# Pair jobs of a streaming-encoder layer: the last half-block sum reads its PSUM bank through VectorE, without a ScalarE copy in between

## The chip, the core and the metric

The kernel runs on one core of a Trainium2 chip. The engines of that core that matter here are TensorE (PE, with its weight loads shown apart as PEld), VectorE (DVE), ScalarE (ACT) and GpSimd (POOL); loads are issued by SyncE (SP) and GpSimd. Each engine works through its own queue in order and waits on semaphores of the others. The metric is the device time of one execution in microseconds, the median of several runs. A profile is of one execution; its span goes from the first to the last instruction.

## What is computed

One layer of an encoder for a sequence of 512 tokens of width 1024: a feed-forward block (FFN 1), a mixer with a recurrent and an attention branch, and a second feed-forward block (FFN 2), with RMS norms around each.

```python
f = swiglu(rms_norm(h, ffn1_pre_g[l]), ffn1_w1[l], ffn1_w3[l], ffn1_w2[l])
h = h + 0.5 * rms_norm(f, ffn1_post_g[l])
u = rms_norm(h, mix_pre_g[l])
q, k, v, xr, xg = jnp.split(u @ w_in[l], splits, axis=-1)
...
y_a = (hr * jax.nn.gelu(xg)) @ w_lru_out[l]
...
g = jax.nn.sigmoid(u @ w_gate[l] + b_gate[l]).reshape(b, s, N_BRANCHES, d)
...
f = swiglu(rms_norm(h, ffn2_pre_g[l]), ffn2_w1[l], ffn2_w3[l], ffn2_w2[l])
h = h + 0.5 * rms_norm(f, ffn2_post_g[l])

def swiglu(x, w1, w3, w2):
    return (jax.nn.silu(x @ w1) * (x @ w3)) @ w2
```

All inputs and outputs are float32. The kernel splits each operand of a product into a high and a low part that TensorE takes in a narrower form of float32, so every product is three matmuls: high x high, low x high, high x low.

## The kernel before

Feature-major products (weights stationary, tokens moving) of a block of 128 features take eight contraction blocks of 128. In most of FFN 1 and FFN 2, in the gelu projection `xg` and in the last two blocks of the gate projection `wg`, two blocks of features are made together as a **pair job**. A job treats the two feature blocks, the two halves of the contraction and the two halves of the tokens as a 2 x 2 matrix product and forms it with seven products instead of eight, each a call of `mm_s` (4 contraction blocks x 3 = 12 matmuls of 128 x 256). Sums of weight blocks are made ahead (S12, S34, by GpSimd or VectorE), sums of the tokens' blocks once per stage (t1 to t4).

The class `Pairs` runs the jobs of FFN 1 (18, w1 and w3 in turn) and FFN 2 (20), `GeluPairs` the four of `xg`, `GatePairs` the one of `wg`: 43 in all. A job holds three PSUM banks, of eight there are:

- `bu` takes a11, and ScalarE copies it out as `q1`; then s2 is added to it, and ScalarE copies that out as `u`; then s3 is added; last, **a22** is added, and what it holds then becomes the left half of the second output block.
- `bx` takes s1, copied out as `q5` by ScalarE; then s4 is added.
- `bc` takes a12.

VectorE makes three sums of them into the job's output tile `c`: bc + q1 (L953), bx + u (L958), and what `bu` holds after s3, plus q5 (L965, in the other two classes L1039 and L1111). `q1`, `q5`, `u` and `v` are quarters of one tile `ct`.

The order on every engine is the order in which the program is written; nothing reorders it. Within a job PE has a11, s1, **the a22 of the job before** (the function `last`), s2, a12, s4, s3. So between s3 and the a22 that adds to the same bank stand 24 matmuls: the a11 and s1 of the next job. In a stage's last job a12 comes after s3 and a22 right after that, so there 12 stand between. In VectorE's queue the third sum comes behind the split of S34 of the next job (`prep(n + 1, 3)`), in ScalarE's queue the copy `v` behind the high half of that split, and in a w3 job of FFN 1 behind the silu of the job before. `prep(n + 1, i)` makes the high parts on ScalarE and the low parts on VectorE (L226 and L227, `split2`).

Tiles come from one pool of 42 equal slots, so a new tile waits for whoever used its slot last. PSUM banks come from a ring of eight.

Of the kernel before, what the change touches and what calls it, by code (L numbers as in the profile page):

```python
# [12 lines left out]
AF = mybir.ActivationFunctionType  # L13
ALU = mybir.AluOpType

P = 128
# [35 lines left out]
def hybrid_layer(ctx: ExitStack, tc: tile.TileContext, a: dict, out: bass.AP):  # L52
    nc = tc.nc
    act, dve, pool, pe, sp = nc.scalar, nc.vector, nc.gpsimd, nc.tensor, nc.sync
# [8 lines left out]
    def slot(shape, dt=F32, name="s"):  # L63
        uid[0] += 1
        return sb.tile(shape, dt, tag="slot", name=f"{name}_{uid[0]}")
# [782 lines left out]
    class Pairs:  # L848
# [65 lines left out]
        def run(self, tail, hooks={}):  # L914
            X = self.X
            assert st["get"] == st["split"] == self.k0, (st, self.k0)
            st["get"] = st["split"] = self.k0 + 2 * len(self.jobs)
            last = silu = lambda: None
            for n, (nm, f) in enumerate(self.jobs):
                W = self.w.pop(n)  # L920
                first = nm == self.na
                tmp = slot([P, 4, 256], name="ct")
                q1, q5, u, v = (tmp[:, i, :] for i in range(4))
                c = slot([P, 2, SEQ], name="cc")
                if first:
                    self.c1[f] = c
                bu, bx, bc = (bank("c")[:, :256] for _ in range(3))
                at = lambda i: [f() for f in hooks.get((n, i), ())]
                mm_s(W["a11"], X["b11"], bu)
                act.activation(q1, bu, AF.Copy)  # L930
                at(1)
                mm_s(W["s1"], X["t1"], bx)
                act.activation(q5, bx, AF.Copy)
                at(2)
                if self.R is not None:
                    self.prep(n + 1, 1)
                silu = last() or silu
                self.prep(n + 1, 1)
                mm_s(W["s2"], X["t2"], bu, True)
                del W["s1"], W["s2"]  # L940
                act.activation(u, bu, AF.Copy)
                at(3)
                if n == len(self.jobs) - 1:
                    silu()
                    silu = lambda: None
                    if self.R is None:
                        tail()
                self.prep(n + 1, 2)

                def c11():  # L950
                    mm_s(W["a12"], X["b21"], bc)
                    del W["a11"], W["a12"]
                    dve.tensor_tensor(out=c[:, 0, :256], in0=bc, in1=q1, op=ALU.add)  # L953

                if n < len(self.jobs) - 1:
                    c11()
                mm_s(W["s4"], X["b22"], bx, True)
                dve.tensor_tensor(out=c[:, 0, 256:], in0=bx, in1=u, op=ALU.add)  # L958
                self.prep(n + 1, 3)
                silu()  # L960
                silu = lambda: None
                mm_s(W["s3"], X["t3"], bu, True)
                del W["s3"], W["s4"]
                act.activation(v, bu, AF.Copy)
                dve.tensor_tensor(out=c[:, 1, 256:], in0=v, in1=q5, op=ALU.add)  # L965
                if n == len(self.jobs) - 1:
                    tail()
                    if self.R is not None:
                        tail()
                    c11()  # L970
                if not first:
                    c1 = self.c1[f]
                    to = self.hid.f
                    to.update((f + i, self.hid.place(f + i, c1[:, i, :])) for i in range(2))
                    dve.tensor_tensor(out=to[f], in0=c1[:, 0, :], in1=c[:, 0, :], op=ALU.mult)
                    dve.tensor_tensor(out=to[f + 1][:, 256:], in0=c1[:, 1, 256:], in1=c[:, 1, 256:], op=ALU.mult)
                self.prep(n + 1, 4)
                self.prep(n + 2, 0)
                self.raws(n + 3)

                def last(W=W, bu=bu, c=c, f=f, first=first):
                    mm_s(W.pop("a22"), X["t4"], bu, True)
                    if first and self.R is not None:
                        act.activation(c[:, 1, :256], bu, AF.Copy)
                        dve.tensor_tensor(out=c, in0=c, in1=self.R, op=ALU.mult)
                        return lambda: act.activation(c, c, AF.Silu)
                    if first:
                        act.activation(c[:, 1, :256], bu, AF.Silu)
                        act.activation(c[:, 0, :], c[:, 0, :], AF.Silu)
                        act.activation(c[:, 1, 256:], c[:, 1, 256:], AF.Silu)  # L990
                    else:
                        c1 = self.c1.pop(f)
                        dve.tensor_tensor(out=self.hid.f[f + 1][:, :256], in0=bu, in1=c1[:, 1, :256], op=ALU.mult)

            last()

    class GeluPairs(Pairs):


        def run(self, scans, yh, yl, tail, between):  # L1000
            X, end = self.X, len(self.jobs) - 1
            assert st["get"] == st["split"] == self.k0, (st, self.k0)
            st["get"] = st["split"] = self.k0 + 2 * len(self.jobs)
            self.raws(2)
            last = mult = parts = lambda: None
            gelu = lambda v: act.activation(v, v, AF.Gelu_apprx_tanh)
            for n, (nm, f) in enumerate(self.jobs):
                W = self.w.pop(n)
                tmp = slot([P, 4, 256], name="ct")
                q1, q5, u, v = (tmp[:, i, :] for i in range(4))  # L1010
                c = slot([P, 2, SEQ], name="cc")
                bu, bx, bc = (bank("c")[:, :256] for _ in range(3))
                mm_s(W["a11"], X["b11"], bu)
                act.activation(q1, bu, AF.Copy)
                mm_s(W["s1"], X["t1"], bx)
                act.activation(q5, bx, AF.Copy)
                self.prep(n + 1, 1)
                between(n)
                last()
                mm_s(W["s2"], X["t2"], bu, True)  # L1020
                act.activation(u, bu, AF.Copy)
                mult()
                self.prep(n + 1, 2)

                def c11():
                    mm_s(W["a12"], X["b21"], bc)
                    dve.tensor_tensor(out=c[:, 0, :256], in0=bc, in1=q1, op=ALU.add)

                if n < end:
                    c11()  # L1030
                mm_s(W["s4"], X["b22"], bx, True)
                dve.tensor_tensor(out=c[:, 0, 256:], in0=bx, in1=u, op=ALU.add)
                parts()
                self.prep(n + 1, 3)
                if n == end:
                    tail()
                mm_s(W["s3"], X["t3"], bu, True)
                act.activation(v, bu, AF.Copy)
                dve.tensor_tensor(out=c[:, 1, 256:], in0=v, in1=q5, op=ALU.add)  # L1039
                if n == end:  # L1040
                    c11()
                gelu(c[:, 0, :])
                if n < end:
                    self.prep(n + 1, 4)
                    self.prep(n + 2, 0)
                self.raws(n + 3)

                def last(W=W, bu=bu, c=c):
                    mm_s(W["a22"], X["t4"], bu, True)
                    act.activation(c[:, 1, :256], bu, AF.Gelu_apprx_tanh)  # L1050
                    gelu(c[:, 1, 256:])

                def mult(c=c, f=f):
                    dve.tensor_tensor(out=c, in0=c, in1=scans[f // 2], op=ALU.mult)

                def parts(c=c):
                    yh.append(slot([P, 2, SEQ], F32R, name="yh"))
                    yl.append(slot([P, 2, SEQ], F32R, name="yl"))
                    split2(yh[-1], yl[-1], c)

            tail()
            last()
            mult()
            parts()

    class GatePairs(Pairs):


        def run(self, gz, bias, tail):
# [3 lines left out]
            last = lambda: None  # L1073
            for n, (nm, f) in enumerate(self.jobs):
                W = self.w[n]
                tmp = slot([P, 4, 256], name="ct")
                q1, q5, u, v = (tmp[:, i, :] for i in range(4))
                c = gz[f // 2] = slot([P, 2, SEQ], name="g")
                bu, bx, bc = (bank("c")[:, :256] for _ in range(3))

# [26 lines left out]
                    tail()  # L1107
                mm_s(W["s3"], X["t3"], bu, True, mark=False)
                del W["s3"], W["s4"]
                act.activation(v, bu, AF.Copy)  # L1110
                dve.tensor_tensor(out=c[:, 1, 256:], in0=v, in1=q5, op=ALU.add)  # L1111
                if n == end:
                    c11()
                gate(c[:, 0, :], 0, 0, SEQ)
# [821 lines left out]
```

## Time and profile before

| | us |
|---|---|
| median of 3 runs (1099.37 to 1099.71) | 1099.57 |
| span of the profiled execution | 1097.6 |
| median less span of the profiled execution | 1.97 |
| PE busy | 1089.0 |
| VectorE busy | 928.9 |
| ScalarE busy | 704.3 |
| GpSimd busy | 420.0 |
| the copies `v` of `Pairs` (38), ScalarE busy | 14.4 |
| the third sums of `Pairs` (38), VectorE busy | 31.3 |

The profiled execution has no device time of its own in the page beside the span; the difference to the median is what lies around the span. Matmuls overlap in the records and their ends are modelled, so the pace of PE is read from the distance between starts. A row of the timeline gives the start and the duration in us, engine, line, operation, output <- input, and in brackets how long the engine was idle before it and on what.

### The profile page before, as it was taken

How to read it: one execution, taken by the hardware profiler on the slowest of the kernel's cores; microseconds unless marked ns; L12 is line 12 of the kernel's file. 1: busy time of each engine (PE TensorE's matmuls, PEld its weight loads, DVE VectorE, ACT ScalarE, POOL GpSimd, SP SyncE). 2: the span in 40 equal slices, each digit the busy share in tenths (PEclk: the TensorE clock that was granted, in tenths of full speed). 3: DMA queues.
4: the chain of work that ended last, by engine and by line, in shares of the span. 5: the costliest groups of instructions: out<-in, count | busy, mean ns of one | idle time of the engine just before them, and what ended most of it. 6: DMA issues, size and time to landing. Idle time of an engine off the chain costs nothing.

```text
span 1097.6 us, 18111 instructions
## 1 busy us (share of the span) xinstructions
PE 1089.0 (99%) x6856; PEld 986.3 (90%) x6856; DVE 928.9 (85%) x1334; ACT 704.3 (64%) x1226; POOL 420.0 (38%) x352
## 2 busy tenths in 40 slices
PE   9999999999999999999999999999999999999997
PEld 7899999998889878899888888888999999998885
DVE  5887999989997998887778867767889989889996
ACT  7756555588767778656656654456555455578872
POOL 0043933232102513242556573010977656633200
PEclk9999999999999999999999999999999999999999
DMA  9325663389866752157132335452423323449923
GB/s 332 129 81 141 127 156 105 110 187 230 231 174 206 166 153 71 39 180 242 60 96 79 113 137 211 138 189 89 123 78 116 110 84 108 147 101 243 206 78 134
DMA packets 53895, 156.46 MB, mean 143 GB/s; under 512 B 5536, under 2 KB 7456, under 8 KB 53808
## 3 DMA queue, kind: packets, MB, share of 16 engines
q1 hardware_dynamic: 40272, 122.49, 33.0%
q0 software_dynamic: 13248, 32.29, 15.6%
q8 instruction: 54, 0.88, 0.3%
q10 hardware_dynamic: 288, 0.52, 0.2%
q14 instruction: 33, 0.27, 0.1%
HBM read 139.57 MB, written 13.62 MB: 140 GB/s over the span
## 4 chain that ended last, share of the span: by engine, by line
PE 99%; DMA 0%; DVE 0%; ACT 0%; issue 0%; DVEq 0%; SPq 0%; ACTq 0%
PE c L842 13%; PE c L843 13%; PE c L844 13%; PE f L237 10%; PE f L238 10%; PE f L239 9%; PE hw L734 6%; PE hw L732 6%; PE hw L733 6%; PE acc L255 1%; PE acc L257 1%; PE acc L256 1%; PE pt L1696 1%; PE s L1660 1%; PE s L1659 1%; PE tr L355 1%
## 5 line engine op out<-in xcount | busy, mean ns | idle before, releaser
L843 PE MATMUL c<-uT,wlo 128*128 128x256 f32 x516 | 146.0, 283 | 0.0
L844 PE MATMUL c<-uT,whi 128*128 128x256 f32 x516 | 146.0, 283 | 0.0
L842 PE MATMUL c<-uT,whi 128*128 128x256 f32 x516 | 146.0, 283 | 0.0
L842 PE MATMUL c<-Xh,whi 128*128 128x256 f32 x504 | 142.7, 283 | 0.0
L843 PE MATMUL c<-Xh,wlo 128*128 128x256 f32 x504 | 142.6, 283 | 0.0
L237 PE MATMUL f<-uT,whi 128*128 128x512 f32 (+1 forms) x380 | 138.5, 365 | 0.0
L238 PE MATMUL f<-uT,wlo 128*128 128x512 f32 (+1 forms) x380 | 136.9, 360 | 0.0
L239 PE MATMUL f<-uT,whi 128*128 128x512 f32 (+1 forms) x380 | 136.9, 360 | 0.0
L844 PE MATMUL c<-Xl,whi 128*128 128x256 f32 x456 | 129.1, 283 | 0.0
L227 DVE TENSOR_TENSOR wlo<-S,whi 128x1024 fp32r<-128x1024 f32 x86 | 121.1, 1408 | 5.9 <-POOL OL L1732 3.1
L226 ACT ACTIVATE whi<-S 128x1024 fp32r<-128x1024 f32 x86 | 88.5, 1054 | 29.8 <-DVE S L891 28.7
L843 PEld LDWEIGHTS c<-uT,wlo 128*128 128x128 f32 x516 | 99.0, 192 | 0.2
L842 PEld LDWEIGHTS c<-uT,whi 128*128 128x128 f32 x516 | 99.0, 192 | 0.2
L844 PEld LDWEIGHTS c<-uT,whi 128*128 128x128 f32 x516 | 99.0, 192 | 0.0
L842 PEld LDWEIGHTS c<-Xh,whi 128*128 128x128 f32 x504 | 96.8, 192 | 0.3 <-issue 0.3
L843 PEld LDWEIGHTS c<-Xh,wlo 128*128 128x128 f32 x504 | 96.8, 192 | 0.0
L732 PE MATMUL hw<-whi,uT 128*128 128x512 f32 x228 | 88.7, 389 | 0.0
L734 PE MATMUL hw<-whi,uT 128*128 128x512 f32 x228 | 88.7, 389 | 0.0
L844 PEld LDWEIGHTS c<-Xl,whi 128*128 128x128 f32 x456 | 87.5, 192 | 0.0
L733 PE MATMUL hw<-wlo,uT 128*128 128x512 f32 x216 | 84.0, 389 | 0.0
L237 PEld LDWEIGHTS f<-uT,whi 128*128 128x128 f32 x380 | 71.8, 189 | 12.1 <-issue 1.7
L239 PEld LDWEIGHTS f<-uT,whi 128*128 128x128 f32 x380 | 71.7, 189 | 11.0
(435 smaller groups left out, 3206.9 us busy)
## 6 DMA issues: line engine op xcount, KB each, us to landing
raw_w1b<-in_w1b_dram SPq DMA_DIRECT2D x22, 512.0 KB, 4.1
raw_w3b<-in_w3b_dram SPq DMA_DIRECT2D x22, 512.0 KB, 4.4
raw_w3a<-in_w3a_dram SPq DMA_DIRECT2D x21, 512.0 KB, 4.9
raw_w1a<-in_w1a_dram SPq DMA_DIRECT2D x20, 512.0 KB, 4.5
raw_w2a<-in_w2a_dram SPq DMA_DIRECT2D x17, 512.0 KB, 6.2
raw_wg<-in_wg_dram SPq DMA_DIRECT2D x16, 512.0 KB, 3.8
raw_w2a<-in_w2a_dram POOLq DMA_DIRECT2D x15, 512.0 KB, 10.2
raw_w2b<-in_w2b_dram SPq DMA_DIRECT2D x15, 512.0 KB, 6.1
```

Of the source, the lines that this page charges most:

```text
L226: act.activation(hi, src, AF.Copy)
L227: dve.tensor_tensor(out=lo, in0=src, in1=f32(hi), op=ALU.subtract)
L237: pe.matmul(ps[:, c0:c1], wh[:, s], h_, start=k == 0 and c0 == 0, stop=False, skip_group_check=True)
L238: pe.matmul(ps[:, c0:c1], wl[:, s], h_, start=False, stop=False, skip_group_check=True)
L239: pe.matmul(ps[:, c0:c1], wh[:, s], l_, start=False, stop=k == KT - 1, skip_group_check=True)
L255: pe.matmul(acc[n], x[:, 0, c], wh[:, s], start=first, stop=False, skip_group_check=skip)
L732: pe.matmul(ps, xs[:, 0, j, c], hi[:, j, :], start=start and j == 0, stop=False, skip_group_check=True)
L733: pe.matmul(ps, xs[:, 0, j, c], lo[:, j, :], start=False, stop=False, skip_group_check=True)
L734: pe.matmul(ps, xs[:, 1, j, c], hi[:, j, :], start=False, stop=i == self.G - 1, skip_group_check=True)
L842: pe.matmul(ps, wh[:, s], xh, start=first, stop=False, skip_group_check=True)
L843: pe.matmul(ps, wl[:, s], xh, start=False, stop=False, skip_group_check=True)
L844: pe.matmul(ps, wh[:, s], xl, start=False, stop=k == 3, skip_group_check=True)
```

## The change

The ScalarE copy of `bu` after s3 is gone, with the quarter `v` of the tile. VectorE's third sum reads the bank itself. This is done in all three classes.

```diff
@@ class Pairs @@
-                tmp = slot([P, 4, 256], name="ct")
-                q1, q5, u, v = (tmp[:, i, :] for i in range(4))
+                tmp = slot([P, 3, 256], name="ct")
+                q1, q5, u = (tmp[:, i, :] for i in range(3))
...
                 mm_s(W["s3"], X["t3"], bu, True)
                 del W["s3"], W["s4"]
-                act.activation(v, bu, AF.Copy)
-                dve.tensor_tensor(out=c[:, 1, 256:], in0=v, in1=q5, op=ALU.add)
+                dve.tensor_tensor(out=c[:, 1, 256:], in0=bu, in1=q5, op=ALU.add)
@@ class GeluPairs @@
-                tmp = slot([P, 4, 256], name="ct")
-                q1, q5, u, v = (tmp[:, i, :] for i in range(4))
+                tmp = slot([P, 3, 256], name="ct")
+                q1, q5, u = (tmp[:, i, :] for i in range(3))
...
                 mm_s(W["s3"], X["t3"], bu, True)
-                act.activation(v, bu, AF.Copy)
-                dve.tensor_tensor(out=c[:, 1, 256:], in0=v, in1=q5, op=ALU.add)
+                dve.tensor_tensor(out=c[:, 1, 256:], in0=bu, in1=q5, op=ALU.add)
@@ class GatePairs @@
-                tmp = slot([P, 4, 256], name="ct")
-                q1, q5, u, v = (tmp[:, i, :] for i in range(4))
+                tmp = slot([P, 3, 256], name="ct")
+                q1, q5, u = (tmp[:, i, :] for i in range(3))
...
                 mm_s(W["s3"], X["t3"], bu, True, mark=False)
                 del W["s3"], W["s4"]
-                act.activation(v, bu, AF.Copy)
-                dve.tensor_tensor(out=c[:, 1, 256:], in0=v, in1=q5, op=ALU.add)
+                dve.tensor_tensor(out=c[:, 1, 256:], in0=bu, in1=q5, op=ALU.add)
```

The order of the instructions shows it at two places of FFN 1. First VectorE around the third sum of a w3 job, before and now; `c_` are PSUM banks, `ct` the tile of q1, q5 and u, `S` the sums of weight blocks, and in brackets stand the engines whose semaphore the row waits for (the number behind the name is the semaphore's own).

```order
L890 TENSOR_TENSOR S_244_1451<-raw_w1a_229_1327,S_243_1450 128x512 [waits Pool_49]
L891 TENSOR_TENSOR S_244_1451<-raw_w1a_229_1327,raw_w1a_230_1329 128x512 [waits DMAHW7_49]
L227 TENSOR_TENSOR wlo_1531<-S_243_1450,whi_1530 128x1024 [waits PE_49,Activation_49]
L953 TENSOR_TENSOR cc_1459<-c_1462,ct_1458 128x256 [waits PE_49]
L958 TENSOR_TENSOR cc_1459<-c_1461,ct_1458 128x256 [waits PE_49]
L227 TENSOR_TENSOR wlo_1561<-S_244_1451,whi_1560 128x1024 [waits Activation_49]
L965 TENSOR_TENSOR cc_1459<-ct_1458 128x256 [waits Activation_49]
L975 TENSOR_TENSOR hEO_1316<-cc_1332,cc_1459 128x512 [waits DVE_49]
```

```order
L890 TENSOR_TENSOR S_244_1444<-raw_w1a_229_1321,S_243_1443 128x512 [waits Pool_49]
L891 TENSOR_TENSOR S_244_1444<-raw_w1a_229_1321,raw_w1a_230_1323 128x512 [waits DMAHW7_49]
L227 TENSOR_TENSOR wlo_1524<-S_243_1443,whi_1523 128x1024 [waits Activation_49]
L953 TENSOR_TENSOR cc_1452<-c_1455,ct_1451 128x256 [waits PE_49]
L958 TENSOR_TENSOR cc_1452<-c_1454,ct_1451 128x256 [waits PE_49]
L227 TENSOR_TENSOR wlo_1554<-S_244_1444,whi_1553 128x1024 [waits Activation_49]
L964 TENSOR_TENSOR cc_1452<-c_1453,ct_1451 128x256 [waits PE_49]
L974 TENSOR_TENSOR hEO_1310<-cc_1326,cc_1452 128x512 [waits DVE_49,Activation_49]
```

The sum keeps its place in the queue; it now reads a bank and waits for PE in place of ScalarE. Lines behind it are one less in the changed file (two or three less in the later classes).

Second, PE where the a22 of that job begins (`Xh`, `Xl` are the split t4, `w` the split weight block a22), before and now:

```order
L842 MATMUL c_1725<-Xh_333,whi_1663 128x256
L843 MATMUL c_1725<-Xh_333,wlo_1664 128x256
L844 MATMUL c_1725<-Xl_334,whi_1663 128x256
L842 MATMUL c_1594<-Xh_549,w_258_1581 128x256 [waits Activation_49]
L843 MATMUL c_1594<-Xh_549,w_258_1581 128x256
L844 MATMUL c_1594<-Xl_550,w_258_1581 128x256
```

```order
L842 MATMUL c_1716<-Xh_333,whi_1655 128x256
L843 MATMUL c_1716<-Xh_333,wlo_1656 128x256
L844 MATMUL c_1716<-Xl_334,whi_1655 128x256
L842 MATMUL c_1586<-Xh_549,w_258_1573 128x256 [waits DVE_49]
L843 MATMUL c_1586<-Xh_549,w_258_1573 128x256
L844 MATMUL c_1586<-Xl_550,w_258_1573 128x256
```

PE's instructions stand as they stood; the first matmul of a22 waits for VectorE where it waited for ScalarE. Elsewhere the order of each engine is the same but for the missing copies, and some first writers of a slot wait for another engine than before, since slots come free in another order.

## The prediction

> **What bounds the kernel now.** I read the page first: busy shares, then the chain that ended last.
>
> ```profile
> span 1097.6 us, 18111 instructions
> ...
> PE 1089.0 (99%) x6856; PEld 986.3 (90%) x6856; DVE 928.9 (85%) x1334; ACT 704.3 (64%) x1226; POOL 420.0 (38%) x352
> ...
> PE 99%; DMA 0%; DVE 0%; ACT 0%; issue 0%; DVEq 0%; SPq 0%; ACTq 0%
> ```
>
> TensorE is both the busiest engine and the whole chain. A busy share can hide short gaps, so next I asked who PE waits for, and what one stretch of pair jobs looks like by windows.
>
> ```profile
> PE w L1152 <- POOL warm L1149: 1.1, 1, 1.1
> PE f L1202 <- ACT uT L1195: 0.4, 1, 0.4
> ...
> 82.50:110.00 27.50, 27.50 (x232) 27.50 (x231) 21.72 (x34) 18.10 (x28) 10.97 (x17) 1.00 0.55 141
> ```
>
> PE's listed waits come to 1.5 us in the whole run, all before the first result. In the window 232 matmuls fill 27.5 us, 119 ns each, at granted clock 1.00. So there is next to no waiting to win back: 1097.6 - 1089.0 = 8.6 us lie outside PE's busy time, in the ramp and after the last matmul, where the change has no instruction. What it can do is make PE wait. The question is therefore the slack of PE against the engine that reads the bank.
>
> **The change part by part.** It removes 43 ScalarE copies (38 + 4 + 1 jobs) and gives 43 VectorE adds a PSUM operand in place of an SBUF one. From the groups by shape, and two lines looked at alone (min/median/max ns):
>
> ```profile
> L964 ACT ACTIVATE ct<-c 128x256 f32<-128x256 f32 x38 | 14.4, 380 | 39.5 <-PE c L844 39.5
> L965 DVE TENSOR_TENSOR cc<-ct 128x256 f32<-128x256 f32 x38 | 31.3, 824 | 1.1 <-ACT ct L964 1.1
> ...
> L965 DVE TENSOR_TENSOR cc<-ct x38: 410/420/1522, 61.1 to 983.5; 128x256 f32<-128x256 f32 x38
> L953 DVE TENSOR_TENSOR cc<-c,ct x38: 404/412/420, 59.3 to 986.1; 128x256 f32<-128x256 f32 x38
> ```
>
> ScalarE loses 43 x 0.38 = 16 us of work, but it sat idle 39.5 us just before those copies, waiting for PE: worth nothing to the end by itself. The new add has the operands of L953 (a bank and ct), which takes 0.41 us every time; the old one took 0.41 to 1.52. So each add costs 0.41 us, at most 1.11 less than before and never more; over the 38 of this line 31.3 - 38 x 0.41 = 16 us less. The Trainium skill (Perfetto Trace Analysis, Optimizing Scalar/DVE Operations) gives VectorE about 60 ns of access overhead on SBUF and 125 on PSUM, and twice that in profiled latency: it speaks against the change, by an estimated 0.13 us per add, and with it the sum below would be about 0.9 us more. L953 against the median of L965 shows no such difference here.
>
> What the change moves is the release of bank bu. The last product of the job, a22 (written one job later), accumulates into bu; its first weight load waits until bu has been read. Before, the reader was ScalarE's copy; now it is VectorE's add, which stands in VectorE's queue behind the split of S34. Behind the waiting weight load stands all of PE's stream. The price of this wait is in the timeline:
>
> ```profile
> 5.72 0.75 DVE L1196 SCALAR_TENSOR_TENSOR uT<-xt,vec,uT 128x512 fp32r<-128x512 f32 x1 [0.40 <-ACT uT L1195]
> 6.53 0.19 PEld L1204 LDWEIGHTS f<-uT,whi 128*128 128x128 f32 x1 [0.49 <-DVE uT L1196]
> ...
> 152.58 0.36 ACT L964 ACTIVATE ct<-c 128x256 f32<-128x256 f32 x1
> ...
> 152.81 0.19 PEld L844 LDWEIGHTS c<-Xl,whi 128*128 128x128 f32 x1
> ...
> 152.99 0.19 PEld L842 LDWEIGHTS c<-Xh,w 128*128 128x128 f32 x1
> 153.05 0.33 PE L842 MATMUL c<-Xh,w 128*128 128x256 f32 x1
> ...
> 153.15 0.41 DVE L965 TENSOR_TENSOR cc<-ct 128x256 f32<-128x256 f32 x1
> ```
>
> The weight load at 6.53 starts 0.06 us after VectorE's 6.47 (its records at full precision: 0.05). At 152.99 the first load of a22 comes 0.18 after the load ahead of it, not 0.12, because the copy ended at 152.94: this job's bank is already released only just in time. And the add, which will now release it, does not end before 153.56. As a load normally starts 0.12 before its matmul, PE is held by (end of add - start of a22's matmul) + 0.05 + 0.12.
>
> Now the places where that is positive. I went through all 43 adds, put 0.41 in for each, and compared with the first matmul of its a22:
>
> ```profile
> 132.89 0.28 PE L842 MATMUL c<-Xh,w 128*128 128x256 f32 x1
> ...
> 132.99 0.41 DVE L965 TENSOR_TENSOR cc<-ct 128x256 f32<-128x256 f32 x1
> ...
> 173.25 0.28 PE L842 MATMUL c<-Xh,w 128*128 128x256 f32 x1
> ...
> 173.35 0.41 DVE L965 TENSOR_TENSOR cc<-ct 128x256 f32<-128x256 f32 x1
> ...
> 230.85 0.34 PE L842 MATMUL c<-Xh,w 128*128 128x256 f32 x1
> ...
> 231.12 0.42 DVE L965 TENSOR_TENSOR cc<-ct 128x256 f32<-128x256 f32 x1
> ...
> 492.02 1.51 DVE L1039 TENSOR_TENSOR cc<-ct 128x256 f32<-128x256 f32 x1
> ...
> 492.42 0.28 PE L842 MATMUL c<-Xh,w 128*128 128x256 f32 x1
> ...
> 509.69 0.42 DVE L1039 TENSOR_TENSOR cc<-ct 128x256 f32<-128x256 f32 x1
> ...
> 509.70 0.28 PE L842 MATMUL c<-Xh,w 128*128 128x256 f32 x1
> ...
> 946.67 0.41 DVE L965 TENSOR_TENSOR cc<-ct 128x256 f32<-128x256 f32 x1
> ...
> 946.75 0.28 PE L842 MATMUL c<-uT,w 128*128 128x256 f32 x1
> ```
>
> - FFN 1, three w3 jobs: 132.99 + 0.41 - 132.89 + 0.17 = **0.68**; the one at 153.05, of which 0.05 is already in the trace, **0.63**; 173.25 again **0.68**.
> - FFN 1, last job, where only c11 (12 matmuls) stands between: 231.54 - 230.85 + 0.17, less 0.06 already there (matmul 0.34 long in place of 0.28): **0.80**.
> - Gelu pairs: 492.43 - 492.42 + 0.17 = **0.18**; the last, again with c11 alone between: **0.58**.
> - FFN 2, one job: 947.08 - 946.75 + 0.17 = **0.50**.
>
> Do they add up, or does VectorE, once PE has stood still, have its lead back? That depends on whether VectorE's lag is tied to PE again in between:
>
> ```profile
> 123.01 0.38 ACT L933 ACTIVATE ct<-c 128x256 f32<-128x256 f32 x1 [1.05 <-PE c L844]
> 123.29 1.05 ACT L226 ACTIVATE whi<-raw_w1a 128x1024 fp32r<-128x1024 f32 x1
> ...
> 124.38 1.23 DVE L227 TENSOR_TENSOR wlo<-raw_w1a,whi 128x1024 fp32r<-128x1024 f32 x1 [0.82 <-ACT whi L226]
> ...
> 144.53 1.23 DVE L227 TENSOR_TENSOR wlo<-raw_w1a,whi 128x1024 fp32r<-128x1024 f32 x1 [0.58 <-ACT whi L226]
> ```
>
> Once per pair of jobs VectorE idles for a ScalarE half whose turn comes after q5, for which ScalarE waits on PE. A PE that is late shifts VectorE there by as much, and the lag builds up anew. So the stalls add. Two more places show a positive number, and drop out:
>
> ```profile
> 111.56 0.60 DVE L965 TENSOR_TENSOR cc<-ct 128x256 f32<-128x256 f32 x1 [0.83 <-ACT ct L964]
> ...
> 122.53 0.41 DVE L965 TENSOR_TENSOR cc<-ct 128x256 f32<-128x256 f32 x1
> ...
> 122.81 0.28 PE L842 MATMUL c<-Xh,w 128*128 128x256 f32 x1
> ...
> 502.50 0.28 PE L842 MATMUL c<-Xh,w 128*128 128x256 f32 x1
> 502.61 0.41 DVE L1039 TENSOR_TENSOR cc<-ct 128x256 f32<-128x256 f32 x1
> ```
>
> The first would cost 122.94 - 122.81 + 0.17 = 0.30, but the add before it no longer waits 0.83 us for a copy, and VectorE doesn't idle between the two; where it stalled all the same, the 0.68 at 132.89 would be that much less, as VectorE is tied to PE ahead of this a22. The second would cost 502.61 + 0.41 - 502.50 + 0.17 = 0.69, but the add before it (492.02) becomes 1.1 us shorter, which its successor should inherit.
>
> Sum: 0.68 + 0.63 + 0.68 + 0.80 + 0.18 + 0.58 + 0.50 = 4.05 us. Against the profiled execution's span this is 1097.6 + 4.05 = 1101.7; its median run is 1099.57, 1.97 above the span, so the time becomes **1103.6**. A stall of under a microsecond cannot be caught up later, as PE has no idle time to give.
>
> Bounds. Below: if the adds at all seven places come 0.7 us earlier than in this trace, nothing is left, 1099.6. Above: twelve further jobs lie within 0.1 us of the condition on one side or the other, for example
>
> ```profile
> 192.87 0.41 DVE L965 TENSOR_TENSOR cc<-ct 128x256 f32<-128x256 f32 x1
> ...
> 193.41 0.28 PE L842 MATMUL c<-Xh,w 128*128 128x256 f32 x1
> ```
>
> (193.28 - 193.41 + 0.17 = 0.04). The removed tile quarter and the vanished reader also alter which released buffer a later tile gets, so some GpSimd sums and loads start at other moments; one VectorE operation that falls on such a sum is 1.1 us longer (L965's 1.52 against 0.41). If that hits four of these jobs, 4 us come on top.
>
> **The rivals.**
> 1. *The stalls vanish: VectorE is relieved.* The adds that took 1.5 us now take 0.41. If that lead is carried to the seven adds, from 0.7 us on, the kernel stays at 1099.6. For it: the 16 us less of VectorE time. Against it: the relief lies in FFN 2 and Gelu, while the four FFN 1 places come after adds that took 0.41 already, with the tie to PE at 124.38 and 144.53 between. A half of the stalls (2 us, 1101.6) is still within what I call no change. 21%.
> 2. *The lag grows.* The shifted GpSimd sums fall on the split ahead of the add in the jobs that are within 0.1 us: 4.05 + 4 = 8 us, 1107.6. For it: the waits of several GpSimd sums do change. Against it: in FFN 1 after 134 us they don't. 18%.
> 3. *Faster.* ScalarE and VectorE together save some 32 us; if PE's pace of 119 ns held waits in it, the pair stages would shorten. At most the 1.5 us of listed waits could go, and they stand ahead of the first pair job: 1098.1 at best, or more only by a pace that no row here shows. 3%.
>
> **How the numbers follow.** The forecast, +3 to +5.5 us, has 58%; with rival 2 it makes slower 76%. Within 0.2% (2.2 us, about what a measurement of this kernel can tell from no change) is rival 1 with its half measure, 21%. The range runs from 1100.2 (a seventh of the stalls left) to 1107.2 (nearly all of rival 2); about 2 in 10 lie outside.
>
> **What would show it right or wrong.** Right: PE's waits list new entries on the add's line, some 0.5 to 0.8 us each, seven or so, near 133, 154, 174, 233, 495, 513 and 950 us (each later by the stalls ahead of it), with an unchanged 119 ns pace between; the add takes 0.41 us everywhere; ScalarE's busy time falls by 16 us, VectorE's by up to as much. Wrong: a first weight load of a22 that starts on time in the w3 jobs of FFN 1 (rival 1), stalls in many other jobs too (rival 2), or a PE wait on a load or a GpSimd sum, which I price at nothing.

## The result, and the profile after

| | before | after |
|---|---|---|
| median of 4 runs each on one chip, us | 1099.47 (1098.90 to 1099.71) | 1104.11 (1103.89 to 1104.34) |
| ratio, 95% interval | | 1.004 (1.0028 to 1.0053) |
| span of the profiled execution, us | 1097.6 | 1101.5 |
| VectorE busy, us | 928.9 | 911.9 |
| ScalarE busy, us | 704.3 | 689.5 |

The kernel became slower by 0.4%, 4.6 us, while two engines did some 32 us less work. The page of the changed kernel, in the same three lines as before:

```profile
span 1101.5 us, 18075 instructions
...
PE 1090.7 (99%) x6856; PEld 986.6 (90%) x6856; DVE 911.9 (83%) x1334; ACT 689.5 (63%) x1183; POOL 422.7 (38%) x352
...
PE 92%; DVE 5%; issue 1%; ACT 1%; DMA 0%; DVEq 0%; SPq 0%; ACTq 0%
```

The busy share of PE still reads 99%. The sign of a change is in the third of them: the chain that ended last now leaves PE and runs through VectorE for 5% of the span. That share is no cost. It says that PE was held by VectorE somewhere, and that the chain then follows VectorE's work back. The waits of PE say where (engine, line and tile that waited, what it waited for: total, times, longest):

```profile
PE c L842 <- DVE cc L964: 1.8, 4, 0.6
PE w L1149 <- POOL warm L1146: 1.1, 1, 1.1
PE f L1199 <- ACT uT L1192: 0.7, 1, 0.7
PE c L842 <- DVE cc L1037: 0.3, 1, 0.3
```

The second and third stand ahead of the first result and were there before (1.1 and 0.4 us). The first and the last are new: L842 is the first matmul of a product, L964 and L1037 are the sum that now reads the bank. Together they come to 2.1 us only, half of what was lost. The reason is seen in the timeline, at the first of these places (start, duration, instruction; in brackets the idle time ahead of it and what ended it):

```profile
132.10 1.21 DVE L227 TENSOR_TENSOR wlo<-S,whi 128x1024 fp32r<-128x1024 f32 x1
...
133.01 0.28 PE L844 MATMUL c<-Xl,whi 128*128 128x256 f32 x1
...
133.23 0.41 DVE L964 TENSOR_TENSOR cc<-c,ct 128x256 f32<-128x256 f32 x1
...
133.70 0.19 PEld L842 LDWEIGHTS c<-Xh,w 128*128 128x128 f32 x1 [0.61 <-DVE cc L964]
...
133.70 0.39 PE L842 MATMUL c<-Xh,w 128*128 128x256 f32 x1 [0.41 <-DVE cc L964]
133.92 0.28 PE L843 MATMUL c<-Xh,w 128*128 128x256 f32 x1
```

The sum stands behind the split of S34 (1.21 us) and ends at 133.64; the first weight load of a22 starts at 133.70, 0.06 later. The view counts idle time from the end of the record at 133.01, whose 0.28 us is a modelled end; PE in fact starts a matmul every 0.12 us. So I took starts: 133.70 - 133.01 is 0.69 where 0.12 is the pace, and the next gap (133.92 - 133.70 = 0.22) is 0.10 long as well. The stall is 0.57 + 0.10 = 0.67 us, where the view gives 0.41.

Measured in this way, the gaps between the matmuls of the pair jobs (what each has over 0.12 us, summed where it is over 0.01) come to 0.11 us before and 4.15 us after. All but 0.03 us of it lies at these places (left out are 0.40 us at 81 us, in both kernels, where two small products of another stage stand between):

| place, us of after | job | stall, us | of it there before |
|---|---|---|---|
| 133.70, 154.53, 175.35 | FFN 1, three w3 jobs | 0.67 each | 0.05, in the second |
| 233.80 | FFN 1, last job | 0.84 | 0.06 |
| 495.50 | Gelu, second job | 0.17 | 0 |
| 505.75 | Gelu, third job | 0.17 | 0 |
| 513.50 | Gelu, last job | 0.56 | 0 |
| 950.82 | FFN 2, one w3 job | 0.37 | 0 |

PE's rows at three of them, the last matmul ahead of a22 and a22's first:

```profile
232.94 0.28 PE L844 MATMUL c<-uT,whi 128*128 128x256 f32 x1
233.80 0.39 PE L842 MATMUL c<-Xh,w 128*128 128x256 f32 x1 [0.58 <-DVE cc L964]
...
505.56 0.28 PE L844 MATMUL c<-wlo,whi 128*128 128x256 f32 x1
505.75 0.39 PE L842 MATMUL c<-Xh,w 128*128 128x256 f32 x1
...
950.43 0.28 PE L844 MATMUL c<-Xl,whi 128*128 128x256 f32 x1
950.82 0.39 PE L842 MATMUL c<-uT,w 128*128 128x256 f32 x1
```

Two of the three carry no wait in brackets, since the modelled end covers it. What gives each of them away is a first matmul of 0.39 us in place of 0.28.

The span grew by 3.9 us, the median by 4.64. Most of the rest lies outside the span. In the four runs of the changed kernel, the time less the span was 2.74 to 2.97 us, against 1.97 in the profiled execution of before; over the 57 runs of the kernel before that accompany the experiments it was 1.83 to 1.96. It is constant for one kernel to about 0.2 us and differs between kernels, so it is no scatter; the trace doesn't reach there, and its cause stays open.

VectorE was relieved of 17.0 us, and it bought nothing. Its groups by shape (busy us, mean ns; idle time ahead), the subtraction of the splits and the sum of FFN 1 and 2 after, then that subtraction before:

```profile
L227 DVE TENSOR_TENSOR wlo<-S,whi 128x1024 fp32r<-128x1024 f32 x86 | 125.6, 1460 | 7.1 <-ACT whi L226 3.8
...
L964 DVE TENSOR_TENSOR cc<-c,ct 128x256 f32<-128x256 f32 x38 | 15.6, 411 | 0.0
```

```profile
L227 DVE TENSOR_TENSOR wlo<-S,whi 128x1024 fp32r<-128x1024 f32 x86 | 121.1, 1408 | 5.9 <-POOL OL L1732 3.1 <-ACT whi L226 2.5
```

The 38 sums fell from 31.3 to 15.6 us, and the subtractions of the splits grew from 121.1 to 125.6. PE was the whole chain before (99%), so work that VectorE is spared counts only where PE waits for VectorE; after the change that is where a sum is late for a22.

### The profile page after: what moved, and what is told of

Read it like the earlier page. It is cut to its first block, busy times and chain, and to the rows that moved or that the text cites. A ratio compares the mean times of both kernels' runs of the same rounds, so it can differ in the third digit from the quotient of the medians.

```text
span 1101.5 us, 18075 instructions
## 1 busy us (share of the span) xinstructions
PE 1090.7 (99%) x6856; PEld 986.6 (90%) x6856; DVE 911.9 (83%) x1334; ACT 689.5 (63%) x1183; POOL 422.7 (38%) x352
## 4 chain that ended last, share of the span: by engine, by line
PE 92%; DVE 5%; issue 1%; ACT 1%; DMA 0%; DVEq 0%; SPq 0%; ACTq 0%
PE c L842 11%; PE c L844 11%; PE c L843 11%; PE f L237 10%; PE f L239 9%; PE f L238 9%; PE hw L734 6%; PE hw L733 6%; PE hw L732 6%; PE acc L257 1%; PE acc L255 1%; PE acc L256 1%; DVE wlo L227 1%; PE pt L1693 1%; PE s L1657 1%
## 5 line engine op out<-in xcount | busy, mean ns | idle before, releaser
L842 PE MATMUL c<-uT,whi 128*128 128x256 f32 x516 | 146.0, 283 | 0.0
L842 PE MATMUL c<-Xh,whi 128*128 128x256 f32 x504 | 142.7, 283 | 0.0
L227 DVE TENSOR_TENSOR wlo<-S,whi 128x1024 fp32r<-128x1024 f32 x86 | 125.6, 1460 | 7.1 <-ACT whi L226 3.8
L842 PEld LDWEIGHTS c<-uT,whi 128*128 128x128 f32 x516 | 99.0, 192 | 0.2
L842 PEld LDWEIGHTS c<-Xh,whi 128*128 128x128 f32 x504 | 96.8, 192 | 0.3 <-issue 0.3
```

The lines of the kernel that those rows point to most:

```text
L227: dve.tensor_tensor(out=lo, in0=src, in1=f32(hi), op=ALU.subtract)
L842: pe.matmul(ps, wh[:, s], xh, start=first, stop=False, skip_group_check=True)
```

## The experiments

The theory: the bank's reader moved from ScalarE, which was early, to VectorE, which is late in a few jobs; PE stalls there by the formula of the prediction. The rivals: that the cost is spread evenly over all 43 jobs, and that it comes from something else that the change does as a whole (the slots, the operand in PSUM). Later runs ask whether the place in the queue or the engine is what counts, and whether PE's pace could gain at all. All ratios are against the kernel before, run alongside on the same chip (its medians were 1099.63 to 1099.70); stalls are PE's, by start to start.

**1. The copy back in eight jobs** (the jobs with a stall; the change stays in 35 of 43).

```diff
-                dve.tensor_tensor(out=c[:, 1, 256:], in0=bu, in1=q5, op=ALU.add)
+                src = bu
+                if n in ((7, 9, 11, 17) if self.R is not None else (15,)):
+                    src = tmp[:, 3, :]
+                    act.activation(src, bu, AF.Copy)
+                dve.tensor_tensor(out=c[:, 1, 256:], in0=src, in1=q5, op=ALU.add)
...
+                if n in (1, 2, 3):
```

The tile has its fourth quarter again here and in experiment 2.

> The change is kept in 35 jobs; the ScalarE copy is put back in the eight whose a22 waits in the profile after (FFN 1: jobs 7, 9, 11, 17 counted from 0; FFN 2: job 15; gelu: 1, 2, 3). Theory A, PE waits for a late VectorE sum at these eight places and nowhere else: the eight stalls (0.67, 0.67, 0.67, 0.84, 0.37, 0.17, 0.17, 0.56 us) go, 1099.5 us, as before the change. Theory B, each sum that reads a bank costs PE or VectorE a little (4.6 us over 43 jobs, 0.11 each): 8/43 of it come back, 1103.2. Theory C, the cost comes from other slots and loads, not from the sums: about 1104.

Measured: 1099.46 us, ratio 0.9998 (0.9989 to 1.0007), stalls 0.11 us in all. PE's waits are those of the start alone:

```profile
PE w L1161 <- POOL warm L1158: 1.1, 1, 1.1
PE f L1211 <- ACT uT L1204: 0.9, 1, 0.9
```

35 copies can go at no cost and for no gain. The whole loss is in these eight jobs.

**2. The change in these eight jobs only.** The same edit with the condition turned round.

> The reverse: the change is made in those eight jobs only, the copy stays in the other 35. Theory A: the same eight stalls, 1103.5 to 1104.3. Theory B: 8/43 of 4.6 us, 1100.3. Theory C: between, as the slots fall, with no stall of a22's first weight load behind a sum.

Measured: 1103.36 us, ratio 1.0033 (1.0020 to 1.0045), just under the range expected. The stalls are those of the changed kernel to 0.01 us but for FFN 2 (0.67 three times, 0.84, 0.17, 0.18, 0.56, and 0.50), 4.25 us in all. PE's waits:

```profile
PE c L842 <- DVE cc L968: 2.0, 5, 0.6
PE w L1161 <- POOL warm L1158: 1.1, 1, 1.1
PE c L842 <- DVE cc L1045: 0.3, 1, 0.3
```

The two runs are complements: eight jobs bring all of the stalls, 35 none. The missing quarter of the tile isn't the cause, since it is back in both. The spans of its runs, 1100.8 to 1101.5, are those of the changed kernel within 0.2 us; the medians differ by what lies outside the span (2.11 to 2.16 us here).

**3. a22 later.** Where the wait of a22 on the sum is the cost, twelve matmuls more ahead of a22 should hide it: the previous job's a22 is put behind s2 in place of ahead of it, in Pairs and in GeluPairs.

```diff
-                silu = last() or silu
                 self.prep(n + 1, 1)
                 mm_s(W["s2"], X["t2"], bu, True)
                 del W["s1"], W["s2"]
                 act.activation(u, bu, AF.Copy)
+                silu = last() or silu
...
-                last()
                 mm_s(W["s2"], X["t2"], bu, True)
                 act.activation(u, bu, AF.Copy)
+                last()
                 mult()
```

> The changed kernel, and in FFN 1, FFN 2 and the gelu jobs the a22 of the job before is issued behind s2, not ahead of it: 36 matmuls (4.3 us) stand between s3 and a22 in place of 24 (2.9 us); a stage's last job keeps its 12. Theory A: the six stalls inside the stages are under 1.44 us each and go (0.67 x 3 + 0.37 + 0.17 x 2 = 2.7 us), the two in last jobs stay (0.84 and 0.56): 1101.4. In FFN 1 the copy of a22 and the product with Rb come 1.44 us later too, so VectorE may lose up to 0.8 us there and a stall of under 0.1 us may be left. Theory B and C: no gain, 1104.

Measured: 1108.15 us, ratio 1.0076 (1.0063 to 1.0090), stalls 8.79 us. This expectation was wrong by 7 us: the kernel became slower than the changed one, where it was to be faster. The stalls ahead of a22 inside the stages did go, but others took their place. PE's waits, new ones among them:

```profile
PE c L842 <- DVE cc L1037: 1.5, 1, 1.5
...
PE c L842 <- DVE cc L964: 1.0, 2, 0.6
PE c L843 <- DVE wlo L227: 1.0, 3, 0.4
PE c L842 <- ACT ct L930: 0.5, 3, 0.2
PE c L842 <- ACT ct L1013: 0.5, 1, 0.5
```

The two ACT entries are s2 waiting for the copy of q1: s2 accumulates into the same bank bu, and a22 had been the cover between s1 and s2. The others are VectorE's, which is now later, because a22's own copy and what hangs on it come later. By starts, s2 behind the copy of q1 makes 3.0 us of the 8.8, low parts of weights that come late from VectorE (L227) 2.4, and the a22 of the last jobs of FFN 1, Gelu and FFN 2 3.4. VectorE and PE around the last Gelu job:

```profile
511.78 1.23 DVE L1052 TENSOR_TENSOR cc<-cc,ig 128x1024 f32<-128x1024 f32 x1 [3.35 <-ACT cc L1005]
512.92 0.42 DVE L1031 TENSOR_TENSOR cc<-c,ct 128x256 f32<-128x256 f32 x1
...
516.41 0.42 DVE L1037 TENSOR_TENSOR cc<-c,ct 128x256 f32<-128x256 f32 x1
...
516.89 0.39 PE L842 MATMUL c<-Xh,w 128*128 128x256 f32 x1 [1.55 <-DVE cc L1037]
```

VectorE, first in first out, idles 3.35 us for the Gelu of the earlier a22, and everything behind the product comes later for it: the third sum ends at 516.83 and a22 starts 0.06 after it. The place of a22 had two jobs, releasing its consumers early and covering q1.

**4. The sum ahead of the split of S34** in Pairs: the sum itself earlier, a22 where it was.

```diff
-                self.prep(n + 1, 3)
                 silu()
                 silu = lambda: None
                 mm_s(W["s3"], X["t3"], bu, True)
                 del W["s3"], W["s4"]
                 dve.tensor_tensor(out=c[:, 1, 256:], in0=bu, in1=q5, op=ALU.add)
+                self.prep(n + 1, 3)
```

> The changed kernel, and in FFN 1 and FFN 2 the third sum stands ahead of the split of S34 for the next job on VectorE (and that split's high half behind s3's place on ScalarE). Theory A: the sum no longer waits behind that split (1.13 us from start to start), which is more than the 0.67 and 0.37 it was late; four stalls go, the last job of FFN 1 (no split ahead of it) keeps 0.84 and the gelu jobs their 0.9: 1104.1 - 2.4 = 1101.7. VectorE now waits for PE at the sum where it was early, up to 0.7 us in FFN 2, which has idle time for it. Rival: in FFN 1 VectorE has no such time and the S34 split comes late for s4: 1104 or more.

Measured: 1101.79 us, ratio 1.0019 (1.0010 to 1.0027), stalls 2.32 us. VectorE and PE at the place of the first timeline:

```profile
131.96 0.41 DVE L963 TENSOR_TENSOR cc<-c,ct 128x256 f32<-128x256 f32 x1
132.29 1.21 DVE L227 TENSOR_TENSOR wlo<-S,whi 128x1024 fp32r<-128x1024 f32 x1
...
132.86 0.28 PE L844 MATMUL c<-Xl,whi 128*128 128x256 f32 x1
132.98 0.28 PE L842 MATMUL c<-Xh,w 128*128 128x256 f32 x1
```

With the sum ahead of the split the bank is free at 132.37, and a22 follows at the pace of 0.12. The three w3 stalls and that of FFN 2 are gone. Left are the last job of FFN 1 (0.84), which has no next job to prepare, so that nothing was moved there, and the Gelu pairs, which the edit leaves alone (0.17, 0.18, 0.56). One is new, 0.57 us at 946.14: the low part of the a11 of a w1 job comes late from VectorE. The rows show where VectorE lost the time: a split at 922.01 that took 1.23 us in the changed kernel took 1.89 here, with a sum of GpSimd beside it until 922.83, and from there to the late split VectorE had no idle time. The four stalls that went say that it is the place in VectorE's queue that costs, not the operand in PSUM.

**5. A late ScalarE copy in the kernel before.** Here VectorE doesn't release the bank at all: the copy stays, and one ScalarE instruction of the next preparation (the high half of w22, 0.61 us) is put ahead of it. The rest of the edit, not shown, lets `prep` make that half alone.

```diff
...
+                wait = n + 1 < len(self.jobs)
+                if wait:
+                    self.prep(n + 1, 4, half=0)
                 act.activation(v, bu, AF.Copy)
                 dve.tensor_tensor(out=c[:, 1, 256:], in0=v, in1=q5, op=ALU.add)
```

> The kernel before, with its ScalarE copy, but in FFN 1 and FFN 2 the copy stands one instruction later in ScalarE's queue, behind the high half of the next job's a22 weights (0.52 us from start to start). VectorE's queue is as before. Theory A, what counts is when bu has been read and not which engine reads it: in jobs 7, 9 and 11 of FFN 1, where the copy was late already, PE waits 132.67 + 0.37 + 0.05 - 132.77 = 0.32, 0.53 and 0.31 us; elsewhere there is room; 1099.5 + 1.15 = 1100.7. Rival, the cost is VectorE's reading of PSUM: no change, 1099.5, and no wait of PE.

Measured: 1100.42 us against 1099.70, ratio 1.0006 (0.9997 to 1.0015). The interval holds no change, so the time alone settles nothing. The trace does: three stalls of 0.29 us at 133.06, 153.50 and 173.95, where 0.32, 0.53 and 0.31 were expected; why the second is no longer than the others stays open. ScalarE and PE at the first (L975 is the copy of bu here):

```profile
132.13 0.61 ACT L870 ACTIVATE w<-raw_w1a 128x512 fp32r<-128x512 f32 x1
132.65 0.36 ACT L975 ACTIVATE ct<-c 128x256 f32<-128x256 f32 x1
...
132.75 0.28 PE L844 MATMUL c<-Xl,whi 128*128 128x256 f32 x1
133.06 0.39 PE L842 MATMUL c<-Xh,w 128*128 128x256 f32 x1
133.29 0.28 PE L843 MATMUL c<-Xh,w 128*128 128x256 f32 x1
```

The copy ends at 133.01, and a22 starts at 133.06 in place of 132.87. The lateness of the reader costs PE, whichever engine reads.

**6. No sum at all.** In the kernel before, ScalarE's copy writes the output tile and the third sum is left out (q5 is missing in the right half of every second block).

```diff
-                act.activation(v, bu, AF.Copy)
-                dve.tensor_tensor(out=c[:, 1, 256:], in0=v, in1=q5, op=ALU.add)
+                act.activation(c[:, 1, 256:], bu, AF.Copy)
...
```

> The kernel before without the third sum: ScalarE copies bu straight into the job's output tile and the 43 VectorE sums are left out, so the right half of every second output block lacks q5. It takes about 33 us of VectorE's busy time away and releases bu as early as before. If PE's pace is its own floor, nothing is gained: 1099.5. Rival, the pace of 119 ns or some later stage holds waits for VectorE: 1 us or more faster, up to 33.

Measured: 1099.30 us against 1099.70, ratio 0.9996 (0.9987 to 1.0005).

```profile
PE 1089.5 (99%) x6856; PEld 986.8 (90%) x6856; DVE 904.5 (82%) x1291; ACT 704.3 (64%) x1226; POOL 419.3 (38%) x352
```

VectorE is 24.4 us less busy and PE's pace is what it was: from its first matmul into tile f to its last PE takes 1084.86 us, 1084.43 before, with 0.11 us of stalls. The interval leaves room for a gain of 1.4 us at most; none shows in PE's rows. The spans of its runs are 0.7 us shorter in the median (1097.1 against 1097.8); in the profiled executions what is shorter is the time ahead of PE's first matmul into f and behind its last matmul, by 0.5 us together.

**7. a22 later in front of the w1 jobs only.** Experiment 3 was two effects in one. Here a22 of the w3 jobs alone moves behind s2.

```diff
-                silu = last() or silu
+                if not first:
+                    silu = last() or silu
...
                 act.activation(u, bu, AF.Copy)
+                if first:
+                    last()
```

> The changed kernel, and in FFN 1 and FFN 2 only the a22 of a w3 job is issued behind s2 of the next job; that of a w1 job and the gelu jobs' stand where they stood. Theory A, with what e3 showed: (1) the a22 of a w1 job feeds the copy and the product with Rb on VectorE, so leaving it early takes away VectorE's wait of 5.0 us at that product and the stalls that came with it; (2) without a22 in between, s2 stands 12 matmuls behind a11, and the copy q1, which ends at 133.27 in the profile after while s2 would begin at 133.13, holds it for 0.31 us in each of jobs 8, 10 and 12. So 3 x 0.67 and 0.37 go, 3 x 0.31 come: 1104.1 - 1.4 = 1102.7. Rival, the loss of e3 came from the later a22 itself, by longer-held banks or by other loads: 1106 or more.

Measured: 1102.38 us, ratio 1.0023 (1.0014 to 1.0032), stalls 3.09 us. The three w3 stalls at a22 go, and s2 waits for q1 in two of those places. ScalarE and PE at the second:

```profile
152.87 0.37 ACT L930 ACTIVATE ct<-c 128x256 f32<-128x256 f32 x1
...
152.98 0.28 PE L844 MATMUL c<-Xl,whi 128*128 128x256 f32 x1
153.28 0.39 PE L842 MATMUL c<-Xh,whi 128*128 128x256 f32 x1
153.51 0.28 PE L843 MATMUL c<-Xh,wlo 128*128 128x256 f32 x1
```

The copy of q1 (L930) ends at 153.24 and s2 starts 0.04 after it, 0.18 late, with 0.11 more in the next gap: 0.29 us. Two stalls of 0.26 to 0.27 appear at the a22 of w1 jobs (122.73 and 204.22), the first of which the prediction had found and dropped. VectorE ahead of it:

```profile
115.57 0.42 DVE L995 TENSOR_TENSOR hEO<-c,cc 128x256 f32<-128x256 f32 x1 [0.20 <-PE c L844]
...
116.51 1.79 DVE L891 TENSOR_TENSOR S<-raw_w3a,raw_w3a 128x512 f32<-128x512 f32 x1
```

VectorE now waits for the later a22 of the w3 job (0.20 us here, 0.24 at the other place), where it did not wait in the changed kernel, and loses the lead that had covered the sum. At the first place a sum of weights takes 1.79 us as well, which took 0.68 in the changed kernel. A third new stall, 0.21 us at 946.54, is a late low part of a11 as in experiment 4.

None of the seven is shown to beat the kernel before; the first is its equal with 35 ScalarE copies fewer.

## Why the prediction was right, step by step

- **PE sets the end and has nothing to give.** Right. Experiment 6 takes the sums away, experiment 1 takes 35 of the copies away, and neither shows a change, since the intervals of both contain 1. Rival 3 (faster) falls: the chain of before left no wait to win.
- **The bank's release moves into VectorE's queue, and PE stands behind it.** Right, and shown from three sides: experiments 1 and 2 tie the whole loss to the eight jobs, 4 removes it where the sum moves up in the queue, 5 makes it with ScalarE as the reader. The rivals fall with 1, 2 and 4: not all the jobs pay, and neither the slots nor the operand as such do.
- **The price, (end of the sum - start of a22) + 0.05 + 0.12.** Right to 0.02 us in six of the seven places. Its 0.17 turned out to be made up otherwise: the restart is 0.06 after the sum, and the next gap is 0.10 longer than the pace.
- **The seven places.** Predicted and measured, in order, as increases: 0.68 and 0.67; 0.63 and 0.62; 0.68 and 0.67; 0.80 and 0.78; 0.18 and 0.17; 0.58 and 0.56; 0.50 and 0.37. In the last, the sum had started 0.08 us ahead of a22's matmul; in the changed kernel it starts at 950.35 and a22 was due at 950.55, a lead of 0.20. By the same formula that is 0.38. The 0.12 us come from one product of VectorE (into hEO): at 924.84 before it took 1.79 us, at 928.63 in the changed kernel 1.66, and VectorE has no idle time from there to the sum. In experiment 2 the product took 1.78, and the stall was 0.50 as predicted.
- **They add up.** Right: 0.67 three times at an interval of 20.8 us, with VectorE tied to PE again in between.
- **The two places dropped.** 122.81 stayed at nothing in the changed kernel, as argued, but with little to spare. Counted against PE, VectorE was 0.9 us ahead at the earlier add and only 0.35 at 114 us, where the 0.30 had to be covered: it did idle in between (0.23 us), and a product that had taken 0.42 us took 1.51. The third Gelu job did not stay at nothing: it cost 0.17 us. The step that failed is "the add before it becomes 1.1 us shorter, which its successor should inherit". The add did become shorter, but the successor inherited 0.5 us of it. VectorE in the changed kernel, with GpSimd's sum beside it:

```profile
495.04 0.41 DVE L1037 TENSOR_TENSOR cc<-c,ct 128x256 f32<-128x256 f32 x1
...
497.92 2.28 POOL L891 TENSOR_TENSOR S<-raw_xg,raw_xg 128x512 f32<-128x512 f32 x1
...
498.97 2.32 DVE L1052 TENSOR_TENSOR cc<-cc,ig 128x1024 f32<-128x1024 f32 x1
...
505.28 0.41 DVE L1037 TENSOR_TENSOR cc<-c,ct 128x256 f32<-128x256 f32 x1
```

and the same product before, where no such sum lay beside it:

```profile
497.41 1.21 DVE L1054 TENSOR_TENSOR cc<-cc,ig 128x1024 f32<-128x1024 f32 x1
```

The 1.1 us that the add at 495 no longer loses to GpSimd is lost again by the product at 499, which now falls on GpSimd's next sum. What was left of the lead took the stall from 0.69 to 0.17. This is read from the rows; no run took that sum away.

- **VectorE gains 16 us, as the sum takes 0.41 everywhere.** Right; the 38 sums of one line by shortest, median and longest:

```profile
L964 DVE TENSOR_TENSOR cc<-c,ct x38: 405/410/419, 60.9 to 987.7; 128x256 f32<-128x256 f32 x38
```

The sum from PSUM never takes longer than 419 ns, where the sum from two SBUF tiles took up to 1522. The Trainium skill (SBUF — State Buffer, Who interferes with whom) says that a VectorE instruction with at most one SBUF input doesn't contend with GpSimd, while one with two contends with a GpSimd instruction that reads SBUF. The row agrees in all 38, of which 19 ran beside some instruction of GpSimd. Of the access overhead that the Trainium skill (Perfetto Trace Analysis, Optimizing Scalar/DVE Operations) sets against PSUM (about 125 ns against 60), nothing shows: 410 ns against the median of 420 from SBUF.

- **Rival 1 (the relief carries VectorE past the stalls)** came true in a part of one place, the third Gelu job. **Rival 2 (the lag grows)** did not come: of the twelve jobs within 0.1 us of the condition, two lose 0.02 and 0.01 us (195.74, the example of the prediction, and 215.91), the others nothing.
- **The sum.** Predicted 4.05 us of stalls; measured 4.15 less 0.11, so 4.04. That it fits so closely is luck: 0.13 too much for FFN 2 and 0.17 too little for Gelu nearly cancel. The span was to be 1101.7 and is 1101.5. The time was to be 1103.6 and is 1104.11, 0.5 above: the term that was off is the 1.97 us outside the span, taken over from before; it is 2.74 to 2.97 in the changed kernel, and no run shows why.

## What to carry to other kernels

When a copy out of PSUM is taken away, ask who now frees the bank, what stands ahead of that reader in its own queue, and how long before the next product into that bank it ends; here some 32 us saved on two engines that had time to spare were worth nothing against 4 us of stalls of the one engine that never waits. With a full engine, go through all the jobs one by one: here 35 of 43 were free, and 8 cost everything. A product that looks movable can be the cover for another wait, as a22 was for the copy of q1; count what it hides before it is moved.

## What the runs showed of the hardware

- A view of PE's waits shows less than the truth: 2.1 us of the 4.15 us lost, because a matmul's recorded end (0.28 us) lies past the start of the next (0.12 us). Starts against starts give it, and a first matmul of 0.39 us marks a restart, even where no wait is listed (experiment 5: 0.88 us lost, none listed).
- After a wait the weight load and its matmul start together, 0.04 to 0.06 us after the release, and the next matmul comes after 0.22 us in place of 0.12. In the runs here this cost 0.10 us on top wherever the first matmul was late by 0.06 us or more; where only its weight load was late, the cost was 0.05 to 0.06 us or less (153.05 and 230.85 in the kernel before).
- Time that one VectorE operation no longer loses can be lost by another: without the sum (experiment 6), which had taken 31.3 us in FFN 1 and 2, the splits of S took 124.2 us in place of 121.1, and in the changed kernel 125.6. VectorE's busy time fell by 24.4 us; a part of that difference is only that neighbouring records overlap (by some 0.07 us a sum).
- The time outside the span belongs to the built kernel: 1.74 to 1.86 us in experiment 1, 2.17 to 2.28 in 6, 2.29 to 2.38 in 3 and 7, 2.74 to 2.97 in the changed kernel. A difference between two kernels of up to 1 us in the median can be this alone; the spans of the runs don't have it.
